# A trunk of two decoder layers on one core: one computed order for all engines, up products with tokens stationary, and seven products of quarters in part of the MLP

## The chip, the cores and the metric

The kernel runs on one core of a Trainium2 chip. The metric is the device time of one execution in microseconds. Work goes to TensorE (PE: matmuls, and PEld: loads of the stationary operand), VectorE (DVE), ScalarE (ACT), GpSimd (POOL) and the queues that issue DMAs, SyncE's (SP) above all.

## The reference, cut to what matters

256 tokens of width 2048 pass two layers, each a token mixer and an MLP on one residual stream.

```python
h = rms_norm(x, mix_norm_g[i])
x = x + (fox_attention if i % 2 == 0 else dilated_attention)(h, ...)
h = rms_norm(x, mlp_norm_g[i])
a = relu(h @ mlp_w_up[i])              # 256x2048 by 2048x8192
x = x + (a * a) @ mlp_w_down[i]        # 256x8192 by 8192x2048
```

Forgetting attention has 16 heads of 128 with normed q and k and a cumulative gate; dilated attention has 8 heads with three groups of q and k each and values of 256. All is float32. Of the multiplications nearly all lie in the projections: 12 + 4 units for the first mixer, 16 + 4 for the second, 32 + 32 for the MLPs, where a unit is 256 tokens by 2048 rows by 512 columns of a weight.

## The kernel before, in words

**Precision by parts.** A float32 operand is cut into a high part that TensorE's fast float32 form takes as it is (ACT casts it, L288) and a low part, the rest (DVE subtracts, L289). A product is three matmuls: high by high, high by low, low by high. The weights come in tiles of 256 rows by 512 columns (`raw`, loaded at L272 on SP's queue), and each tile is cut as a whole, 128x1024 per operation. Here such a tile is called a block pair, as it has two blocks of 128 rows (k). There are five buffers of raw tiles and five of cut ones.

**Three forms of product.** `product` (L317 to L319) keeps 128 tokens stationary and moves 512 weight columns: per k, two token halves by three matmuls of 512 columns. `product_transposed` (L365, L369) is used for the up projections: it keeps 128 weight columns stationary and moves tokens, so that its result already stands with hidden units on partitions, as the down projection needs it. Per k it takes four times one matmul of 512 columns (high weights by high and low tokens side by side) and one of 256. `last_product` (L343 to L345) is the last unit of all: it ends in parts, so that its additions and stores overlap, and its second half of tokens is in two runs of matmuls of 256 columns.

**An MLP** goes in four periods of 2048 hidden units: four up units, then four down units. `up_chain` (L842 to L852) adds the two halves of each bank, squares the positive part and cuts the result; the scale of the norm is applied as its square when the down product is added to x (L805).

**Order.** Python generators (`Jobs`) write the order by hand: each k step of a product is one tick, after which generators that have waited so many ticks emit their next instructions. What stands between the projections' matmuls on TensorE is attention (scores, transposes of probabilities, products with values) and transposes of normed tokens. Three of four chunks of a norm are turned from tokens on partitions to width on partitions by DVE in 32x32 squares (L399) and a way through DRAM (four writes and one read per 128 tokens); the last chunk by TensorE (L434). Queries and keys are turned through DRAM too (the reads on POOL's queue), except for two blocks by TensorE (L506). `behind` adds dependencies that fix one instruction behind another.

**Head.** The first weight tile comes in two loads of 256 KB on two queues and is cut in two halves (L915, L916).

Of the kernel before, what the change touches and what calls it, by code (L numbers as in the profile page):

```python
# [23 lines left out]
KC = D // P  # L24
DFF = 4 * D
# [9 lines left out]
RAW_BUFS = 5  # L35
W_BUFS = 5
W_SUB = 2
RAW_SUB = 2


class Jobs:

    def __init__(self):
        self.now = 0
        self.live = []
        self.done = set()  # L50
        self.running = False

    def spawn(self, gen):
        self.live.append([self.now, None, gen])
        if not self.running:
            self._run()

    def _run(self):
        self.running = True
        for job in list(self.live):  # L60
            while job[0] <= self.now and (job[1] is None or job[1] in self.done):
                try:
                    got = next(job[2])
                except StopIteration:
                    self.live.remove(job)
                    break
                if isinstance(got, int):
                    job[0], job[1] = self.now + got, None
                    if not got:
                        continue  # L70
                else:
                    job[1] = got
        self.running = False

    def tick(self):
        self.now += 1
        self._run()

    def need(self, key):
        tries = 0  # L80
        while key not in self.done:
            self.tick()
            tries += 1
            assert tries < 10000, key
# [3 lines left out]
def trunk(ctx: ExitStack, tc, x, fox_w_in, fox_b_f, fox_q_gain, fox_k_gain, fox_w_out, dil_w_in,  # L88
          dil_q_gain, dil_k_gain, dil_w_out, mix_norm_g, mlp_norm_g, mlp_w_up, mlp_w_down, out):
    nc = tc.nc  # L90
    jobs = Jobs()

    const = ctx.enter_context(tc.tile_pool(name="const", bufs=1))
    act = ctx.enter_context(tc.tile_pool(name="act", bufs=1))
    wpool = ctx.enter_context(tc.tile_pool(name="wpool", bufs=1))
    work = ctx.enter_context(tc.tile_pool(name="work", bufs=1))
    small = ctx.enter_context(tc.tile_pool(name="small", bufs=8))
    dram = ctx.enter_context(tc.tile_pool(name="dram", bufs=1, space=bass.MemoryType.DRAM))
    ps_acc = ctx.enter_context(tc.tile_pool(name="ps_acc", bufs=4, space=PSUM))
    ps_tp = ctx.enter_context(tc.tile_pool(name="ps_tp", bufs=2, space=PSUM))  # L100
    ps_sc = ctx.enter_context(tc.tile_pool(name="ps_sc", bufs=2, space=PSUM))


    warm = small.tile([P, 1], F32, tag="warm", name="warm", bufs=1)
    nc.gpsimd.memset(warm, 0.0)
    nc.scalar.activation(warm, warm, AF.Exp)
    ident = const.tile([P, P], F32, name="ident")
    make_identity(nc, ident)
    mhalf = const.tile([P, 8], F32, name="mhalf")
    nc.gpsimd.memset(mhalf, -0.5)  # L110


    spare = ps_sc.tile([P, P], F32, tag="sc", name="spare")

    def wake(times):
        for _ in range(times):
            nc.tensor.transpose(spare, ident, ident)

    wake(8)


    gain = const.tile([P, 4 * KC + 8], F32, name="gain")
    MLP_G, FOX_G, DIL_G = 2 * KC, 4 * KC, 4 * KC + 2

    def gain_rows(name, sources):
        rows = work.tile([2 * KC, P], F32, tag="s", name=name, bufs=4)
        at = 0
        for src in sources:
            nc.sync.dma_start(rows[at:at + src.shape[0], :], src)
            at += src.shape[0]  # L130
        return rows[0:at, :]

    def gain_columns(name, rows, at):
        n = rows.shape[0]
        ps = ps_tp.tile([P, 512], F32, tag="tp", name=f"ps_{name}")
        nc.tensor.transpose(ps[:, :n], rows, ident[:n, :n])
        return nc.vector.tensor_copy(gain[:, at:at + n], ps[:, :n])

    per_chunk = "l (c p) -> (l c) p"
    mix_rows = gain_rows("g_mix", [mix_norm_g.rearrange(per_chunk, p=P)])  # L140


    xt = [act.tile([P, NT, NC], F32, tag=f"x{n}", name=f"x{n}") for n in range(NX)]
    xv = x[0].rearrange("(t p) d -> p t d", p=P)


    bf = const.tile([P, FH], F32, name="bf")
    wfs = work.tile([P, KC, 2 * FH], F32R, tag="t1", name="wfs")
    tables = {}

    def distances():

        di = work.tile([P, 3 * P], I32, tag="s", name="di", bufs=4)
        nc.gpsimd.iota(di[:, 0:P], pattern=[[-1, P]], base=0, channel_multiplier=1)
        nc.gpsimd.iota(di[:, P:3 * P], pattern=[[-1, 2 * P]], base=P, channel_multiplier=1)
        return di

    def more_constants():
        yield 9
        wf = work.tile([P, KC, FH], F32, tag="t2", name="wf")  # L160
        with behind(issued["load"]):
            nc.sync.dma_start(wf, fox_w_in[0][:, 3 * D:3 * D + FH].rearrange("(c p) n -> p c n", p=P))
            nc.sync.dma_start(bf, fox_b_f.to_broadcast([P, FH]))
            qk_rows = gain_rows("g_qk", [fox_q_gain, fox_k_gain, dil_q_gain[0], dil_k_gain[0]])
            mlp_rows = gain_rows("g_mlp", [mlp_norm_g.rearrange(per_chunk, p=P)])
        di = distances()
        yield 6
        with behind(*issued["n0"]):
            nc.scalar.copy(wfs[:, :, 0:FH], wf)
            nc.vector.tensor_sub(wfs[:, :, FH:2 * FH], wf, wfs[:, :, 0:FH].bitcast(F32))  # L170
        jobs.done.add("wf")
        yield 1
        gain_columns("g_qk", qk_rows, FOX_G)
        for c in (FOX_G, DIL_G, DIL_G + 1, DIL_G + 2):
            nc.vector.tensor_scalar_mul(gain[:, c:c + 1], gain[:, c:c + 1], SCALE)
        yield 1
        gain_columns("g_mlp", mlp_rows, MLP_G)
        yield 1
        mask = work.tile([P, 3 * P], F32, tag="t0", name="mask")
        nc.vector.tensor_copy(mask, di)  # L180
        nc.vector.tensor_scalar(mask, mask, 0.0, None, ALU.is_ge)
        nc.vector.tensor_scalar(mask, mask, BIG, -BIG, ALU.mult, ALU.add)
        tables["mask"] = mask
        jobs.done.add("mask")

    def dilation_tables():
        di = distances()
        yield 2
        df = work.tile([P, 3 * P], F32, tag="s", name="df", bufs=4)
        nc.vector.tensor_copy(df, di)  # L190
        for g, r in enumerate(DILATION):
            t = work.tile([P, 3 * P], F32, tag=f"t{g}", name=f"dist{g}")
            ok = work.tile([P, 3 * P], F32, tag="s", name=f"ok{g}", bufs=4)
            nc.vector.tensor_scalar(ok, df, 0.0, None, ALU.is_ge)
            nc.vector.tensor_scalar(t, df, float(SPAN * r), None, ALU.is_le)
            nc.vector.tensor_mul(ok, ok, t)
            yield 1
            if r > 1:
                ri = work.tile([P, 3 * P], I32, tag="s", name=f"ri{g}", bufs=4)
                nc.vector.tensor_scalar(ri, di, r - 1, None, ALU.bitwise_and)  # L200
                nc.vector.tensor_copy(t, ri)
                nc.vector.tensor_scalar(t, t, 0.0, None, ALU.is_equal)
                nc.vector.tensor_mul(ok, ok, t)
                yield 1
            nc.vector.tensor_mul(t, df, ok)
            nc.vector.tensor_scalar(ok, ok, -BIG, BIG, ALU.mult, ALU.add)
            nc.vector.tensor_add(t, t, ok)
            tables[g] = t
            jobs.done.add(("table", g))
            yield 1  # L210


    plan = []

    def add(w, rows, cols):

        for r in range(rows[0], rows[1], RAW_SUB * P):
            plan.append((w, r, cols))

    for j in range(4):  # L220
        for part in range(3):
            add(fox_w_in[0], (0, D), [(part * D + j * NC, NC)])
    for n in range(NX):
        add(fox_w_out[0], (0, D), [(n * NC, NC)])

    def add_mlp(l):
        for b in range(4):
            for n in range(4):
                add(mlp_w_up[l], (0, D), [(b * D + n * NC, NC)])
            for n in range(NX):  # L230
                add(mlp_w_down[l], (b * D, (b + 1) * D), [(n * NC, NC)])

    add_mlp(0)
    for q4 in range(4):
        for g in range(3):
            c = g * DH * P + q4 * 2 * P
            add(dil_w_in[0], (0, D), [(c, 2 * P), (3 * DH * P + c, 2 * P)])
        add(dil_w_in[0], (0, D), [(6 * DH * P + q4 * NC, NC)])
    for n in range(NX):
        add(dil_w_out[0], (0, D), [(n * NC, NC)])  # L240
    add_mlp(1)

    issued = {}

    def behind(*instructions):
        stack = ExitStack()
        for i in instructions:
            stack.enter_context(tc.issue_after(getattr(i, "ins", i)))
        return stack

    def hold(first):

        if "held" not in issued:
# [737 lines left out]
```

## Time and profile before

| what | value |
|---|---|
| time, median of 3 runs (lowest to highest) | 2164.76 us (2164.07 to 2165.49) |
| profiled execution, first to last instruction | 2163.6 us |
| PE, PEld busy | 2153.5, 1918.3 us |
| DVE, ACT, POOL busy | 1395.5, 1108.1, 70.8 us |
| granted TensorE clock | 1.000 |
| moved by DMA | 454.11 MB |

The profiled execution's own time was not taken apart from its span; the median of the runs lies 1.2 us above the span. Matmuls overlap each other in the rows (a start every 0.2 us, a duration of 0.38), so PE's busy share says that something was in flight, not how fast the matmuls followed each other. For that, starts are compared.

### The profile page before, as it was taken

What the parts mean: (1) busy time and instruction counts of PE and PEld (TensorE: products, weight loads), DVE (VectorE), ACT (ScalarE), POOL (GpSimd) and SP (SyncE); (2) the same over time, 40 slices, a digit from 0 to 9 for tenths busy, and PEclk for the clock granted to TensorE, in tenths of its full rate; (3) what the DMA queues carried; (4) which work ended last, traced back from release to release, by engine and by line L of the source; (5) the groups of instructions that cost most, each with busy time, mean ns of one, the idle gap of its engine ahead of it and who ended that gap; (6) DMA issues with size and microseconds to landing.
All of it is one profiled execution on the core that took longest, in us unless ns stands there. A gap on an engine that the chain in (4) does not pass through costs nothing.

```text
span 2163.6 us, 30020 instructions
## 1 busy us (share of the span) xinstructions
PE 2153.5 (100%) x11251; PEld 1918.3 (89%) x11251; DVE 1395.5 (64%) x1847; ACT 1108.1 (51%) x1536; POOL 70.8 (3%) x87
## 2 busy tenths in 40 slices
PE   9999999999999999999999999999999999999999
PEld 8888888998998998998888888888988988988988
DVE  6777796665665565566667777766655655655664
ACT  6655655544444454455555555655544543544542
POOL 1111000000000000000010010000000000000000
PEclk9999999999999999999999999999999999999999
DMA  8676658666666766767776776767666666666764
GB/s 253 219 224 190 222 175 264 200 202 202 201 203 203 200 201 204 203 199 242 216 251 204 242 224 198 240 203 237 203 204 201 199 204 204 200 202 203 203 211 140
DMA packets 285683, 454.11 MB, mean 210 GB/s; under 512 B 21144, under 2 KB 99040, under 8 KB 285536
## 3 DMA queue, kind: packets, MB, share of 16 engines
q1 hardware_dynamic: 282240, 442.36, 65.7%
q0 software_dynamic: 2880, 9.44, 1.2%
q8 instruction: 88, 1.44, 0.3%
q10 hardware_dynamic: 416, 0.39, 0.1%
q14 instruction: 59, 0.48, 0.1%
HBM read 435.86 MB, written 16.25 MB: 209 GB/s over the span
## 4 chain that ended last, share of the span: by engine, by line
PE 95%; DVE 2%; ACT 1%; DMA 1%; issue 1%; POOL 0%; SPq 0%; ACTq 0%; DVEq 0%; POOLq 0%
PE acc L318 20%; PE acc L319 20%; PE acc L317 20%; PE up_n3a_acc L365 5%; PE up_n1a_acc L365 5%; PE up_n3a_tp L365 3%; PE up_n3a_sc L365 3%; PE up_n1a_tp L365 3%; PE up_n1a_sc L365 3%; PE up_n1a_acc L369 3%; PE up_n3a_acc L369 3%; PE up_n1a_sc L369 1%; PE up_n3a_sc L369 1%; PE up_n1a_tp L369 1%; PE up_n3a_tp L369 1%; DVE wl L289 1%
## 5 line engine op out<-in xcount | busy, mean ns | idle before, releaser
L289 DVE TENSOR_TENSOR wl<-raw,wh 128x1024 fp32r<-128x1024 f32 x799 | 974.8, 1223 | 692.2 <-ACT wh L288 690.1
L288 ACT CAST wh<-raw 128x1024 fp32r<-128x1024 f32 x799 | 837.2, 1048 | 924.1 <-PE acc L319 591.7
L317 PE MATMUL acc<-wh,hT_n 128*128 128x512 f32 x896 | 344.4, 385 | 0.0
L318 PE MATMUL acc<-wl,hT_n 128*128 128x512 f32 x896 | 340.1, 380 | 0.1
L319 PE MATMUL acc<-wh,hT_n 128*128 128x512 f32 x896 | 340.0, 380 | 0.0
L317 PE MATMUL acc<-wh,aTh_n1a 128*128 128x512 f32 x512 | 194.0, 379 | 0.0
L318 PE MATMUL acc<-wl,aTh_n1a 128*128 128x512 f32 x512 | 194.0, 379 | 0.0
L319 PE MATMUL acc<-wh,aTl_n1a 128*128 128x512 f32 x512 | 194.0, 379 | 0.0
L319 PEld LDWEIGHTS acc<-wh,hT_n 128*128 128x128 f32 x896 | 169.6, 189 | 24.1
L317 PEld LDWEIGHTS acc<-wh,hT_n 128*128 128x128 f32 x896 | 170.0, 190 | 22.6 <-ACT hT_n L440 0.7
L318 PEld LDWEIGHTS acc<-wl,hT_n 128*128 128x128 f32 x896 | 169.9, 190 | 22.3 <-DVE wl L289 0.5
L317 PE MATMUL acc<-wh,aTh_n3a 128*128 128x512 f32 x480 | 181.9, 379 | 0.0
L318 PE MATMUL acc<-wl,aTh_n3a 128*128 128x512 f32 x480 | 181.9, 379 | 0.0
L319 PE MATMUL acc<-wh,aTl_n3a 128*128 128x512 f32 x480 | 181.9, 379 | 0.0
L365 PE MATMUL up_n1a_acc<-hT_n,wh 128*128 128x512 f32 x512 | 181.6, 382 | 0.0
L365 PE MATMUL up_n3a_acc<-hT_n,wh 128*128 128x512 f32 x512 | 181.6, 382 | 0.0
L369 PE MATMUL up_n1a_acc<-hT_n,wl 128*128 128x256 f32 x512 | 139.6, 273 | 0.0
L369 PE MATMUL up_n3a_acc<-hT_n,wl 128*128 128x256 f32 x512 | 139.6, 273 | 0.0
L318 PEld LDWEIGHTS acc<-wl,aTh_n1a 128*128 128x128 f32 x512 | 96.8, 189 | 13.8
L319 PEld LDWEIGHTS acc<-wh,aTl_n1a 128*128 128x128 f32 x512 | 96.8, 189 | 13.7
L317 PEld LDWEIGHTS acc<-wh,aTh_n1a 128*128 128x128 f32 x512 | 96.8, 189 | 13.6
L365 PEld LDWEIGHTS up_n1a_acc<-hT_n,wh 128*128 128x128 f32 x512 | 96.8, 189 | 13.5
(730 smaller groups left out, 3209.4 us busy)
## 6 DMA issues: line engine op xcount, KB each, us to landing
raw<-in_mlp_w_up_dram SPq DMA_DIRECT2D x256, 512.0 KB, 4.0
raw<-in_mlp_w_down_dram SPq DMA_DIRECT2D x256, 512.0 KB, 3.7
raw<-in_dil_w_in_dram SPq DMA_DIRECT2D x192, 256.0 KB, 3.2
raw<-in_fox_w_in_dram SPq DMA_DIRECT2D x95, 512.0 KB, 4.1
raw<-in_fox_w_out_dram SPq DMA_DIRECT2D x32, 512.0 KB, 3.9
raw<-in_dil_w_in_dram SPq DMA_DIRECT2D x32, 512.0 KB, 6.6
raw<-in_dil_w_out_dram SPq DMA_DIRECT2D x32, 512.0 KB, 4.5
blocks_n<-turned_n SPq DMA_DIRECT2D x72, 64.0 KB, 1.9
```

Source lines behind the costliest of these rows:

```text
L288: issued["cast"] = nc.scalar.copy(hi, raw)
L289: issued["cut"] = nc.vector.tensor_sub(lo, raw, hi.bitcast(F32))
L317: nc.tensor.matmul(acc[t], ah[:, tok], hi, start=first, stop=False)
L318: nc.tensor.matmul(acc[t], ah[:, tok], lo, start=False, stop=False)
L319: issued["product"] = nc.tensor.matmul(acc[t], al[:, tok], hi, start=False, stop=last)
L365: issued["product"] = nc.tensor.matmul(banks[b], hi[:, i, col], in_turn(tokens.rearrange("p x s -> p (x s)"), P // 2), start=first, stop=last)
L369: nc.tensor.matmul(banks[b][:, 0:S], lo[:, i, col], in_turn(tokens[:, 0, :], P // 2), start=False, stop=False)
```

## The change

Nearly every line of the kernel is rewritten.

- **Order.** Each step is entered in a `Plan` with its engine, an estimated duration, what it reads and writes. `Plan.order` works backwards to a due time for each step, then runs a model of the five engines and the DMA queue three times, taking at each moment the ready step that is due first (attention's matmuls, marked urgent, before all). The instructions are then emitted in the order of the modelled times. Buffers are rings with fixed slots, and four phases share the memory.
- **Up products** keep tokens stationary, as all others. Their result has tokens on partitions: it is evacuated, scaled by the norm and passed through relu on ACT, turned by DVE (one operation of 1024) and through DRAM, squared, cast and cut.
- **Seven products of quarters.** In periods 1, 2 and 3 of both MLPs, in pairs 0, 2, 4, 5 and 7 of each up unit, the 256 tokens by 256 rows by 512 columns are taken as a 2x2 by 2x2 block product with sums of blocks (seven products instead of eight, each 128 tokens by 128 rows by 256 columns, three matmuls each). The other three pairs of those units use the same banks by quarters: eight products of 256 columns. In period 0 and in the down units nothing is halved.
- **Interleaving.** In periods 1 to 3, each up unit alternates with a down unit of the period before, pair by pair.
- **All norms' chunks** and all queries and keys after the first norm are turned through DRAM, on SP's queue.
- First units of a stage go in couples: six pairs of one, six of the other, then the two last pairs of each.
- The weights' first load is one of 512 KB. Buffers: six raw tiles and four cut pairs, one more of each in the MLPs.

```diff
+FIVE = (0, 2, 4, 5, 7)
+HALVED = [[(), (), (), ()], [FIVE] * 4, [FIVE] * 4, [FIVE] * 4]
...
+def moved(kb):
+    return kb / 380.0
...
+    HANDOFF = 0.25
+    LANDING = 2.1
...
+        def quarters(self, raw, keys, j, first, last):
+            q = S
+            hi, lo = cut(raw, keys, 0, 2 * NC, j in self.adding)
+            for i in range(2):
...
+                    for t in range(NT):
+                        a, b = (self.source.at(k, x, t) for x in range(2))
+                        for half in range(2):
+                            h, l = (in_turn(r(w)[:, i * NC + half * q:i * NC + (half + 1) * q], P) for w in (hi, lo))
+                            for m, w in ((a, h), (a, l), (b, h)):
+                                nc.tensor.matmul(to[t, half], m, w, start=False, stop=False)
...
+        def parts(self, raw, keys, j, first, last):
+            q = S
+            sums = raw_ring.take()
+            add("dve", on_dve(2 * q), lambda: nc.vector.tensor_add(
+                v(sums)[:, 0:2 * q].rearrange("p (g n) -> p g n", g=2),
+                v(raw)[:, q:3 * q].rearrange("p (g n) -> p g n", g=2),
+                v(raw)[:, 0:q].unsqueeze(1).to_broadcast([P, 2, q])), reads=keys, writes=[(sums, 0)])
+            hi_w, lo_w = cut(raw, keys, q, 3 * q)
+            add("dve", on_dve(q), lambda: nc.vector.tensor_add(v(sums)[:, 2 * q:3 * q], v(sums)[:, 0:q], v(raw)[:, 2 * q:3 * q]),
+                reads=[(sums, 0), *keys], writes=[(sums, 1)])
+            add("dve", on_dve(q), lambda: nc.vector.tensor_add(v(sums)[:, 3 * q:4 * q], v(sums)[:, 2 * q:3 * q], v(raw)[:, 3 * q:4 * q]),
+                reads=[(sums, 1), *keys], writes=[(sums, 2)])
+            hi_s, lo_s = cut(sums, [(sums, i) for i in range(3)], 0, 4 * q)
...
+                rows = [[(q1q5[:, 0:q], own(0, 0), pure, 0, 1), (q2q6[:, 0:q], own(1, 0), pure, 2, 1),
+                         (q3[:, 0:q], lambda x: at_sigma(x, 3), pure, 1, 3)],
+                        [(q1q5[:, q:2 * q], lambda x: at_sigma(x, 0), summed, 0, 2), (q7q4[:, 0:q], lambda x: at_sigma(x, 2), summed, 1, 1),
+                         (q2q6[:, q:2 * q], lambda x: at_sigma(x, 1), summed, 2, 2), (q7q4[:, q:2 * q], own(1, 1), summed, 3, 2)]]
+                for acc, a, w, at, edge in rows[summing]:
+                    nc.tensor.matmul(acc, a(0), w(0, at), start=first and edge & 1 == 1, stop=False)
+                    nc.tensor.matmul(acc, a(0), w(1, at), start=False, stop=False)
+                    nc.tensor.matmul(acc, a(1), w(0, at), start=False, stop=last and edge & 2 == 2)
...
+    def through_dram(turned, into, size=NT * NC):
+        blocks = blocks_ring.take()
+        for i in range(4):
+            def go(i=i):
+                nc.sync.dma_start(v(blocks)[:, :, :, i, :].rearrange("t j c x -> c t j x"),
+                                  v(turned)[32 * i:32 * i + 32, 0:size].rearrange("p (t j x) -> p t j x", t=NT, j=4))
+            add("dma", 0.45, go, reads=[turned], writes=[(blocks, i)])
...
+        add("dma", moved(512), back, reads=[(blocks, i) for i in range(4)], writes=[into])
...
+                for b_, to, at, names in pairs:
...
+                            nc.scalar.copy(flat(at()), two(v(b_)))
+                    add("act", on_act(NC), go, reads=[b_], writes=[(to, x) for x in names])
...
+                        nc.scalar.activation(at, at, AF.Relu, scale=by(t))
...
+            add("dve", 1.4, lambda: nc.vector.transpose(
+                v(turned).rearrange("p (t j b r) -> p t b j r", t=NT, j=4, b=4),
+                v(z)[:, 0:2 * NC].rearrange("p (t b j c) -> p t b j c", t=NT, j=4, c=32)),
+                reads=[(z, t) for t in range(NT)], writes=[turned, z])
+            through_dram(turned, z)
...
+    AC, BE = ("A0", "A1", "C0", "C1"), ("B0", "B1")
+    UU_D = "UUDUDUDUDUDUDUDD"
...
+                for u, d in zip(ups, downs):
+                    for c in UU_D:
+                        (u if c == "U" else d).block()
```

1722 lines of the change are left out of this document (945 added, 777 removed).

## Prediction

> **What bounds the kernel now.** I read the page first, then the two stretches of the trace that matter (projections alone, and attention), then single rows.
>
> ```profile
> span 2163.6 us, 30020 instructions
> PE 2153.5 (100%) x11251; PEld 1918.3 (89%) x11251; DVE 1395.5 (64%) x1847; ACT 1108.1 (51%) x1536; POOL 70.8 (3%) x87
> PEclk9999999999999999999999999999999999999999
> PE 95%; DVE 2%; ACT 1%; DMA 1%; issue 1%; POOL 0%; SPq 0%; ACTq 0%; DVEq 0%; POOLq 0%
> ```
>
> TensorE has a matmul in flight for 2153.5 of 2163.6 us at full clock, and 95% of the chain that ended last is its own work. So the time is the number of matmuls times their distance from start to start. Busy time cannot give that distance, since matmuls overlap; I take it from first and last rows of runs in the timeline. The columns are start, duration, engine, line.
>
> ```profile
> 1000.00 0.38 PE L317 MATMUL acc<-wh,aTh_n1a 128*128 128x512 f32 x1
> ...
> 1005.83 0.38 PE L317 MATMUL acc<-wh,aTh_n1a 128*128 128x512 f32 x1
> ```
> ```profile
> 449.91 0.38 PE L365 MATMUL up_n1a_acc<-hT_n,wh 128*128 128x512 f32 x1
> ...
> 452.20 0.38 PE L365 MATMUL up_n1a_tp<-hT_n,wh 128*128 128x512 f32 x1
> ```
> ```profile
> 2153.95 0.27 PE L343 MATMUL last<-wh,aTh_n3a 128*128 128x256 f32 x1
> ...
> 2159.20 0.28 PE L345 MATMUL last<-wh,aTl_n3a 128*128 128x256 f32 x1
> ```
>
> Down-type run: 27 steps in 5.83 us, 0.2159 us for 512 columns. Up run: seven couples of 512 and 256 columns in 2.29 us, 0.327 us a couple. Run of 256 columns alone: 47 steps in 5.25 us, **0.1117 us**, not half of 0.2159. This last row prices the change.
>
> Check of the whole: 68 units (of 2048 rows by 512 columns) with 96 matmuls of 512, less the 48 that the last unit splits: 6480 x 0.2159 = 1399; up, 32 units x 64 couples x 0.327 = 670; the split ones 11. Sum 2080. The other 84 us are attention, transposes, head, tail and short stalls.
>
> ```profile
> 660.00:990.00 330.00, 330.00 (x1778) 296.35 (x1777) 195.04 (x209) 152.12 (x176) 0.00 (x0) 1.00 0.66 202
> ```
> ```profile
> 40.00:320.00 280.00, 276.65 (x1389) 243.43 (x1388) 215.14 (x405) 166.01 (x295) 31.51 (x34) 1.00 0.65 204
> ```
> ```profile
> 1100.00:1400.00 300.00, 300.00 (x1483) 264.89 (x1482) 221.46 (x319) 172.76 (x260) 28.75 (x30) 1.00 0.72 226
> ```
>
> The stretches give length, PE, PEld, DVE, ACT, POOL busy, clock, DMA. In an MLP, VectorE is busy 59% (195 of 330); in the two attention stages 77% and 74%, and TensorE still loses only 3.35 us and 0.
>
> **The change, part by part.** *Matmuls.* A block pair is 256 rows by 512 columns. Up before: 8 couples, 8 x 0.327 = 2.617 us. After, in period 0 of each MLP (64 pairs): 12 x 0.2159 = 2.591. In periods 1 to 3, 72 pairs by quarters, 24 x 0.1117 = 2.681, and 120 pairs by seven products, 21 x 0.1117 = 2.346. Before 256 x 2.617 = 670.0; after 165.8 + 193.0 + 281.5 = 640.3. **Term 1: -29.7 us.** The saving of one eighth of the columns in 120 pairs is 39 us at half of 0.2159 each; a quarter of it goes to the dearer 256-column matmul.
>
> The Trainium skill, "TensorE: Matmul & The Clock Gate", section "LDWEIGHTS (loading the stationary operand)", puts a load of 128 columns at columns / 1.2, 107 ns, and its section "Back-to-back issue gap" a matmul of 256 columns at 262 cycles, 109 ns, so the load would just hide. The run above shows 0.1117, so the trace does not agree; by the pages Term 1 would be some 11 us larger.
>
> *Transposes on TensorE that go* to DMA: 24 of the norms before the two MLPs and the dilated layer, 16 of two key blocks.
>
> ```profile
> 384.24 0.44 PE ptx_n L434 x4
> ...
> 1390.80 0.44 PE tq_('dqk', 3, 2)_1_12903 L506 x4
> ```
>
> Ten groups of four at 0.44: **Term 2: -4.4 us.** What waits next there is the turn by DMA: the last chunk of a norm is now wanted only after twelve block pairs (31 us), and the turn takes two landings (rows below) and some 8 us of engine work, about 15.
>
> *VectorE in periods 1 to 3.* One up unit is interleaved with one down unit: 16 pairs. TensorE: 8 x 2.591 + 3 x 2.681 + 5 x 2.346 = 40.5 us (before 8 x 2.591 + 8 x 2.617 = 41.7); 24 such groups, 972 us. VectorE's own rate, start to start, from rows where it was never kept waiting:
>
> ```profile
> 1189.09 0.70 DVE L529 STREAM_TRANSPOSE sq_('dqk', 1, 1)_0_10872<-qn_('dqk', 1, 1)_0_10916 128x512 f32<-128x512 f32 x1
> 1189.71 0.67 DVE L529 STREAM_TRANSPOSE sq_('dqk', 1, 1)_1_10874<-qn_('dqk', 1, 1)_1_10919 128x512 f32<-128x512 f32 x1
> 1190.31 3.45 DVE L289 TENSOR_TENSOR wl<-raw,wh 128x1024 fp32r<-128x1024 f32 x3
> ```
> ```profile
> 301.36 0.75 DVE L579 TENSOR_TENSOR oTfl<-po_f,oTfh 128x256 fp32r<-128x256 f32 x2
> 302.02 0.41 DVE L589 TENSOR_TENSOR pTl_f<-ptp_f,pTh_f 128x256 fp32r<-128x256 f32 x1
> ```
> ```profile
> 320.54 1.28 DVE L807 TENSOR_TENSOR x<-x,acc 128x512 f32<-128x512 f32 x2
> ```
> ```profile
> L289 DVE TENSOR_TENSOR wl<-raw,wh 128x1024 fp32r<-128x1024 f32 x799 | 974.8, 1223 | 692.2 <-ACT wh L288 690.1
> L852 DVE TENSOR_TENSOR aTl_n3a<-z_n3a,aTh_n3a 128x512 fp32r<-128x512 f32 x32 | 21.8, 680 | 0.0
> ```
>
> 1024 elements: (3.45 - 1.23) / 2 = 1.11; 512: 1.28 - 0.68 = 0.60; 256: 0.66 / 2 = 0.33; 768 between: 0.86; a turn of 512: 0.62, so of 1024 some 1.2. A pair by seven products takes an addition of 512, a cut of 768, two additions of 256 and a cut of 1024: 0.60 + 0.86 + 0.66 + 1.11 = 3.23. Per group: 11 plain cuts 12.2; five such pairs 16.2; the end of the up unit and the addition to x 5.9 (0.60 + 0.66 + 1.20 in additions, turn 1.20, cut 1.11, x 1.11). Sum 34.3.
>
> ```profile
> 1145.50 0.54 DVE L773 TENSOR_TENSOR p_d<-sd 128x384 f32<-128x384 f32 x1
> 1146.07 0.56 DVE L774 TENSOR_TENSOR p_d<-p_d,sd 128x384 f32<-128x384 f32 x1
> 1146.55 1.22 DVE L289 TENSOR_TENSOR wl<-raw,wh 128x1024 fp32r<-128x1024 f32 x1
> ```
>
> An operation that reads its predecessor's result starts 0.57 after it, an independent one 0.48: 0.1 for each of some 14 dependent steps, 1.4. **VectorE needs 35.7 of 40.5 us, 88%**: it fits, above the 77% that cost nothing or little. It comes in bursts: at the start of a group, two up pairs and a down pair (7.6 us of TensorE) meet 5.5 us of cuts and most of the 5.9, a lag of about 3 us. Cover: five pairs of cut buffers. A group of one seven-product pair and one down pair takes three buffers in 4.94 us, so a buffer comes round in 8.2 us; the cut takes 2.6 (ScalarE 1.06, VectorE 1.23, handoffs), the matmuls on it 1.7 on average, leaving 3.9. Lag and cover nearly match. **Term 3**, stall in these 972 us: between the dilated stage's share, 0, and the attention stage's, 3.35 / 280 = 1.2%, or 11.6 us. I take the middle, **+5.8**, since some of the 3.35 belongs to attention's own chain. If the cover is gone each group loses the lag, 3 x 24 = 72 us. Below zero is excluded: 330.00 of 330.00 leaves nothing to regain.
>
> *ScalarE*, same group: 16 casts of 1024, five of 768, eight passes of 512, one more cast.
>
> ```profile
> L288 ACT CAST wh<-raw 128x1024 fp32r<-128x1024 f32 x799 | 837.2, 1048 | 924.1 <-PE acc L319 591.7 <-PE up_n1a_acc L365 150.1 <-PE up_n3a_acc L365 150.0
> L851 ACT CAST aTh_n3a<-z_n3a 128x512 fp32r<-128x512 f32 x32 | 20.0, 624 | 4.5 <-DVE z_n3a L848 4.4
> ```
>
> 17 x 1.05 + 5 x 0.84 + 8 x 0.62 = 27 of 40.5 us. The up unit has one set of four banks; its four evacuating passes (2.5 us) lie beside two down pairs (5.2 us). Nothing.
>
> *DMA.* Each up unit now goes through DRAM, four writes of 128 KB and one read of 512 KB, all on SP's queue between the weight loads.
>
> ```profile
> raw<-in_mlp_w_up_dram SPq DMA_DIRECT2D x256, 512.0 KB, 4.0
> ...
> blocks_n<-turned_n SPq DMA_DIRECT2D x72, 64.0 KB, 1.9
> turned_n<-blocks_n SPq DMA_DIRECT2D x18, 256.0 KB, 3.8
> ```
>
> 32 MB on 454, and the reads of the 20 query and key turns come from POOL's queue to SP's; per group five issues beside 16 loads. A read that waits for its writes holds the loads behind it for 2 us; seven raw buffers give 10 us and more. The turned result is wanted after 30 us or more. I cost it at nothing; if the cover went, a load would come 2 us late, once in a group: 48 us.
>
> *Attention under a computed order.* The same matmuls, placed between projections by estimated times instead of counted steps. Nothing in the trace shows such an order: a gain is at most the 3.35 us above, a loss as in the rivals. I take 0, by the dilated row.
>
> *Head.* First weights come in one load of 512 KB, not two of 256, so the first cast and cut are twice as long.
>
> ```profile
> 4.60 0.62 ACT L915 CAST wh<-raw 128x512 fp32r<-128x512 f32 x1 [1.84 <-DMA raw<-in_fox_w_in_dram]
> 5.25 0.69 DVE L916 TENSOR_TENSOR wl<-raw,wh 128x512 fp32r<-128x512 f32 x1 [0.82 <-ACT wh L915]
> ...
> 6.98 0.80 PE L317 MATMUL acc<-wh,hT_n 128*128 128x512 f32 x1
> ```
>
> 1.05 + 1.23 against 0.62 + 0.69: **Term 4: +1.0** (0 to 4, a late landing). The tail keeps its form: 0.
>
> Sum: 2163.6 - 29.7 - 4.4 + 5.8 + 1.0 = 2136.3. The median of the runs is 1.2 above the profiled span: **2137.5**.
>
> **The rivals.** *A, cheap quarters.* If 256 columns cost half of 512, 0.108, the 4248 of them (1728 and 2520) would save 16 us more than Term 1: 2121. For: in the up run a 256 beside a 512 adds 0.327 - 0.216 = 0.111, no more. Against: the run at 0.1117.
>
> *B, a stiff order.* In-order queues hold what stands behind a result that lands late. One load of 512 KB in the dilated stage took a median of 6.6 us:
>
> ```profile
> raw<-in_dil_w_in_dram SPq DMA_DIRECT2D x32, 512.0 KB, 6.6
> ```
>
> The order counts on 1.35 + 2.1 and one more us for a turned tile: 2.2 late. Behind 64 turns (32 up, 12 norm, 20 heads) at a third of that uncovered: +47 at worst, half of it likely: 2150 to 2163. Against: the consumers have ready work before and behind them.
>
> *C, slower: VectorE becomes the bound.* In the seven-product pair the second cut needs the third addition, then ScalarE's cast (1.06), then VectorE. If the queue holds nothing ready there, VectorE idles:
>
> ```profile
> 43.22 1.06 ACT wh L288
> 44.28 0.02 issue
> 44.30 1.23 DVE wl L289
> ```
>
> 1.08 each, 5.4 a group, and 2.4 at the unit's end (two passes of 0.62 before the turn, a cast before the last cut). All exposed: 35.7 + 7.8 = 43.5 us a group, +72: 2205. It costs nothing below 40.5 and turns the change slower from 40.5 + 33.1 / 24 = 41.9, that is with 6.2 of the 7.8 exposed. Taken most exposed, 2185. For: 88% and a lag like the cover. Against: the rows of three and four operations with no gap, wherever the queue has other work.
>
> The Trainium skill, "VectorE: DVE Perf Modes", section "The DRAIN you can't avoid", says that the next operation does not start until the pipe is empty, which speaks for C. The trace disagrees: three cuts in 3.45 us start 0.11 before their predecessor ends. By that rule the mean durations would add, 38.6 + 1.4 = 40.0 us a group, and no lag could be made up.
>
> **How the numbers follow.** Forecast (2125 to 2150) 0.63; A (2125 or less) 0.10; B 0.14, some of it within 0.2% or 4.3 us of before (about what a measurement of this kernel can tell from no change); C 0.13. Faster 0.83, same 0.04, slower 0.13. Range 2117 to 2168: A below, without Term 3's stall in part (2121 - 4), C from its threshold above; left out are 0.03 and 0.12.
>
> **What would show it.** Right: seven-product runs at 0.1117 a step; VectorE near 88% in the periods 1 to 3 with TensorE above 99% of its own rate; no group L434 or L506 after the head. Wrong: 0.108 a step (A); idle time of TensorE or VectorE ended by a DMA of a turned tile (B); VectorE's cut of the sums waiting on ScalarE while TensorE waits on that cut (C).

## The result, and the profile after

| | median | lowest to highest | profiled span |
|---|---|---|---|
| before, same chip | 2164.66 us | 2164.07 to 2165.49 | 2163.6 |
| changed | 2133.57 us | 2132.18 to 2134.92 | 2130.8 |

The ratio is 0.9856, with a 95% interval of 0.9842 to 0.9870: 31.1 us faster. The forecast was 2137.5, 3.9 too high. The page of the changed kernel, its total, engines and clock, then the shares of the chain that ended last:

```profile
span 2130.8 us, 32094 instructions
PE 2117.1 (99%) x12125; PEld 1917.1 (90%) x12125; DVE 1669.3 (78%) x2092; ACT 1263.0 (59%) x1640; POOL 57.3 (3%) x51
PEclk9999999999999999999999999999999999999999
PE 95%; DMA 2%; DVE 1%; issue 1%; ACT 1%; SPq 0%; DVEq 0%; ACTq 0%
```

VectorE has 274 us more to do and ScalarE 155 more, yet the chain is TensorE's as before. The time fell mainly because TensorE's own work became shorter. Its matmuls became more (12125 against 11251), many of them half as wide. The stretches of the changed kernel (length, PE, PEld, DVE, ACT, POOL busy, clock, DMA share, GB/s) show how well it is kept supplied:

```profile
460.00:860.00 400.00, 400.00 (x2705) 374.77 (x2705) 351.16 (x429) 251.59 (x295) 0.00 (x0) 1.00 0.72 233
40.00:320.00 280.00, 280.00 (x1417) 247.90 (x1416) 206.44 (x340) 156.02 (x253) 22.90 (x14) 1.00 0.68 212
1100.00:1400.00 300.00, 300.00 (x1482) 265.08 (x1481) 221.89 (x292) 169.21 (x242) 19.91 (x10) 1.00 0.71 227
```

The first line lies in periods 1 to 3 of an MLP: VectorE 351.16 of 400, 87.8%, and TensorE is never without a matmul. Nor did the matmuls follow each other more slowly than forecast: a group of 273 in 40.5 us would give 2696 in 400 us, and 2705 are there. The second is the first attention stage, in which 3.35 us had been lost before. Now the steps themselves, the changed kernel's timeline on TensorE (start, duration). A pair by quarters is followed by a down pair of 512 columns:

```profile
463.47 0.28 PE L403 MATMUL bank_C<-hi,hT 128*128 128x256 f32 x1
...
466.15 0.38 PE L384 MATMUL bank_E<-mlp_hi,aT 128*128 128x512 f32 x1
...
467.88 0.38 PE L386 MATMUL bank_E<-mlp_hi,aT 128*128 128x512 f32 x1
```

From 463.47 to 466.15 stand the 24 matmuls of a pair: 0.1117 us each, while the eight steps that follow take 1.73 us, 0.216 each. As before, half the columns take more than half the time.

What TensorE waits for over the whole span, in the changed kernel (us in total, times, longest), and then in the kernel before:

```profile
PE bank_E L666 <- DMA fox_s<-in_mix_norm_g_dram: 2.2, 1, 2.2
PE bank_B L384 <- DVE x L523: 2.0, 1, 2.0
PE bank_E L697 <- DMA x<-in_x_dram: 1.7, 1, 1.7
...
PE bank_A L384 <- issue: 1.4, 1, 1.4
PE bank_B L1192 <- DVE x L1207: 0.8, 1, 0.8
PE bank_A L384 <- ACT aT L642: 0.5, 1, 0.5
PE bank_C L403 <- DVE mlp_lo L346: 0.2, 1, 0.2
```
```profile
PE po_f L576 <- DVE pTl_f L589: 2.2, 3, 0.7
...
PE pc L674 <- DVE g_lf L671: 1.1, 1, 1.1
...
PE sc_d L610 <- DVE sd L759: 0.2, 1, 0.2
```

Attention's waits (2.2, 1.1 and 0.2, all of the kernel before) are gone but for 0.5 (aT L642). The MLPs' cuts cost 0.2 in all. In their place two things got worse. The head, in the timeline of TensorE:

```profile
6.75 0.31 PE L666 MATMUL bank_E<-ident,fox_s 32*128 32x32 f32 x1 [2.23 <-DMA fox_s<-in_mix_norm_g_dram]
8.78 1.09 PE L697 MATMUL bank_E<-ident,x 128*128 128x128 f32 x4 [1.72 <-DMA x<-in_x_dram]
9.51 0.78 PE L384 MATMUL bank_A<-hi,hT 128*128 128x512 f32 x1
```

The first product starts at 9.51, not 6.98, after waits for the gain rows and for the second half of x. That the gain rows do not set its start is shown by e9_wide_joints below. And the joints between stages, all engines:

```profile
378.18 0.45 PE L384 MATMUL bank_A<-mlp_hi,hT 128*128 128x512 f32 x1 [1.36 <-issue]
1030.62 1.21 DVE L523 TENSOR_TENSOR x<-x,bank_B 128x1024 f32<-128x1024 f32 x1
1031.97 0.45 PE L384 MATMUL bank_B<-hi,hT 128*128 128x512 f32 x1 [1.98 <-DVE x L523]
```

At 1031.97 the dilated stage begins on the bank pair that the MLP's last unit has just filled, and waits until VectorE has added that unit to x. At 378.18 it is the same with bank A after the first mixer's last unit. The two cost 1.36 and 1.98 us, and the last unit 0.8 more (L1192 in the waits). Behind the second one the granted clock is 0.50 for 3.4 us (row in the last section), some 1.7 us more.

### The profile page after: what moved, and what is told of

It is laid out like the page before. It is cut to its first block, busy times and chain, and to the rows that moved or that the text cites. A ratio compares the mean times of both kernels' runs of the same rounds, so it can differ in the third digit from the quotient of the medians.

```text
span 2130.8 us, 32094 instructions
## 1 busy us (share of the span) xinstructions
PE 2117.1 (99%) x12125; PEld 1917.1 (90%) x12125; DVE 1669.3 (78%) x2092; ACT 1263.0 (59%) x1640; POOL 57.3 (3%) x51
## 2 busy tenths in 40 slices
DMA packets 336140, 493.04 MB, mean 231 GB/s; under 512 B 21928, under 2 KB 137712, under 8 KB 335984
## 4 chain that ended last, share of the span: by engine, by line
PE 95%; DMA 2%; DVE 1%; issue 1%; ACT 1%; SPq 0%; DVEq 0%; ACTq 0%
PE bank_B L384 11%; PE bank_B L386 11%; PE bank_B L385 11%; PE bank_A L384 7%; PE bank_A L386 7%; PE bank_A L385 7%; PE bank_C L403 7%; PE bank_E L384 5%; PE bank_E L386 5%; PE bank_E L385 5%; PE bank_A L434 2%; PE bank_A L433 2%; PE bank_A L432 2%; PE bank_A L403 2%; PE bank_C L434 2%; PE bank_C L432 2%
## 5 line engine op out<-in xcount | busy, mean ns | idle before, releaser
L340 ACT CAST hi<-raw 128x1024 fp32r<-128x1024 f32 (+1 forms) x720 | 734.9, 1026 | 618.9 <-PE bank_B L386 211.5
L346 DVE TENSOR_TENSOR lo<-raw,hi 128x1024 fp32r<-128x1024 f32 (+1 forms) x720 | 852.7, 1192 | 295.4 <-ACT hi L340 283.2
L384 PE MATMUL bank_A<-hi,hT 128*128 128x512 f32 x520 | 199.2, 383 | 0.0
L384 PE MATMUL bank_B<-hi,hT 128*128 128x512 f32 x512 | 196.8, 384 | 2.0 <-DVE x L523 2.0
L386 PE MATMUL bank_A<-hi,hT 128*128 128x512 f32 x520 | 197.7, 380 | 0.0
L384 PE MATMUL bank_B<-hi,aT 128*128 128x512 f32 x520 | 197.7, 380 | 0.0
L385 PE MATMUL bank_A<-lo,hT 128*128 128x512 f32 x520 | 197.6, 380 | 0.0
L385 PE MATMUL bank_B<-lo,aT 128*128 128x512 f32 x520 | 197.1, 379 | 0.0
L386 PE MATMUL bank_B<-hi,aT 128*128 128x512 f32 x520 | 197.1, 379 | 0.0
L386 PE MATMUL bank_B<-hi,hT 128*128 128x512 f32 x512 | 194.8, 380 | 0.0
L385 PE MATMUL bank_B<-lo,hT 128*128 128x512 f32 x512 | 194.7, 380 | 0.0
L384 PE MATMUL bank_E<-hi,aT 128*128 128x512 f32 x408 | 154.8, 379 | 0.0
L386 PE MATMUL bank_E<-hi,aT 128*128 128x512 f32 x408 | 154.6, 379 | 0.0
L346 DVE TENSOR_TENSOR mlp_lo<-raw,mlp_hi 128x1024 fp32r<-128x1024 f32 (+1 forms) x108 | 126.9, 1175 | 32.8 <-ACT mlp_hi L340 29.7
L386 PEld LDWEIGHTS bank_A<-hi,hT 128*128 128x128 f32 x520 | 98.5, 189 | 14.5 <-DVE hT L707 0.5
L384 PEld LDWEIGHTS bank_A<-hi,hT 128*128 128x128 f32 x520 | 98.8, 190 | 13.2
```

Of the source, the lines that this page charges most:

```text
L340: add("act", on_act(n), lambda: nc.scalar.copy(r(hi)[:, 0:n], v(src)[:, at:at + n]), reads=keys, writes=[hi])
L346: add("dve", on_dve(n), lambda: nc.vector.tensor_sub(r(lo)[:, 0:n], v(src)[:, at:at + n], v(hi)[:, 0:n]), reads=[*keys, hi], writes=[lo])
L384: nc.tensor.matmul(acc, a, h, start=first and i == 0, stop=False)
L385: nc.tensor.matmul(acc, a, l, start=False, stop=False)
L386: nc.tensor.matmul(acc, b, h, start=False, stop=last and i == 1)
```

## The experiments

Each kernel was timed in five rounds beside the kernel before. Each is the changed kernel with the edit shown. First the size of the main term.

**No seven products** (e1_none).

```diff
-HALVED = [[(), (), (), ()], [FIVE] * 4, [FIVE] * 4, [FIVE] * 4]
+HALVED = [[()] * 4] * 4
```

> The changed kernel with no unit by seven products: all up units as whole products of 512 columns, the computed order, the tokens stationary and the turns by DMA as they are. Theory (the time is the sum of matmul steps, VectorE has room): 120 pairs cost 2.591 in place of 2.346 us, +29.4, and 72 pairs 2.591 in place of 2.681, -6.5: +22.9, so 2156.5. The rest of the change is then worth -8 against the kernel before. Rival (the gain comes from the computed order and the lost transposes, the seven products being eaten by the dearer small matmuls and by VectorE): within 5 us of the changed kernel, 2129 to 2139.

Measured: 2154.08 (2152.35 to 2155.10), ratio 0.9946 (0.9933 to 0.9958). So halving brings 20.5 of the 31.1 us. The step lengths of 0.2159 and 0.1117 give 23.0 for it (192 x 2.591 less 193.0 and 281.5). The other 10.6 us stay without any halving: 6.7 of them are the up products with tokens stationary by the same step lengths (256 x 2.617 less 256 x 2.591).

**Quarters as wide matmuls** (e2_wide). The accumulators are laid out anew so that the quarters that stand side by side share a bank; the three pairs of a unit that are not by seven products then take 512 columns at a time.

```diff
-                        for half in range(2):
-                            h, l = (in_turn(r(w)[:, i * NC + half * q:i * NC + (half + 1) * q], P) for w in (hi, lo))
-                            for m, w in ((a, h), (a, l), (b, h)):
-                                nc.tensor.matmul(to[t, half], m, w, start=False, stop=False)
+                        h, l = (in_turn(r(w)[:, i * NC:(i + 1) * NC], P) for w in (hi, lo))
+                        to = (q3q2, q0q4)[t]
...
+                                nc.tensor.matmul(to, m, w, start=False, stop=False)
```

> The accumulators lie so that the two column halves of one token half are neighbours in a bank, and the three other pairs of each halved unit are six matmuls of 512 columns a block in place of twelve of 256: same columns, half the number. Theory (a matmul of 256 columns alone costs 0.1117, more than half of 0.2159, as it is paced by something that counts matmuls, not columns): 72 pairs x (2.681 - 2.591) = -6.5, 2127.1. Rival (columns alone count): the same time, 2133.6.

Measured: 2125.86 (2123.95 to 2127.32), ratio 0.9814 (0.9800 to 0.9827): 7.7 us off for the same multiplications. 72 pairs at 2.681 less 2.591 give 6.5. The edit also gives the planner 6 x 0.216 for half such a pair in place of 12 x 0.109, so the order may have moved a little too. Against e1_none, which has no seven products and the same wide matmuls, the run is 28.2 us faster, and the 120 pairs by seven products had been priced at 29.4. A matmul has a price besides its columns. The Trainium skill, "TensorE: Matmul & The Clock Gate", section "Back-to-back issue gap", gives 109 ns for 256 columns, by which 24 of them would take 2.62 us and the edit would bring about 2 us, an estimate; the measurement speaks for 0.1117.

Next, how much room VectorE still has, and what ends it.

**All eight pairs, and six** (e3_eight, e4_six).

```diff
-FIVE = (0, 2, 4, 5, 7)
+FIVE = (0, 1, 2, 3, 4, 5, 6, 7)
```

> All eight pairs of the halved units by seven products. TensorE would need 39.5 us a group of 16 pairs, VectorE 8 x 1.11 + 8 x 3.23 + 5.9 + 2.0 = 42.6. Theory (VectorE bounds from about 40.5 us a group): a group takes 42.6 in place of 40.4, 24 x 2.2 = +53, 2186; at the least slower than the changed kernel. Rival (VectorE is far from its bound, its rows overlap more than worked out): 72 x 0.335 = -24, 2109.5.

```diff
-FIVE = (0, 2, 4, 5, 7)
+FIVE = (0, 2, 3, 4, 6, 7)
```

> Six of the eight pairs (0, 2, 3, 4, 6, 7) by seven products. TensorE 40.1 us a group, VectorE 10 x 1.11 + 6 x 3.23 + 5.9 + 1.6 = 38.0, 95%. Theory (VectorE fits while its need is below TensorE's): 24 x 0.335 = -8.0, 2125.6. Rival (88% with bursts is already the edge, the five cut buffers don't cover a longer lag): up to 1 us lost a group, 2133 to 2150.

Measured: eight 2238.10 (2229.56 to 2243.55), ratio 1.0329 (1.0307 to 1.0351); six 2153.92 (2151.14 to 2157.51), ratio 0.9946 (0.9933 to 0.9958). At eight the direction is the theory's and the loss larger. The stretch of eight, then of six, in the same columns as above:

```profile
460.00:860.00 400.00, 369.37 (x2338) 341.36 (x2337) 365.55 (x496) 240.32 (x288) 0.00 (x0) 0.95 0.67 210
```
```profile
460.00:860.00 400.00, 390.33 (x2590) 362.82 (x2589) 359.17 (x454) 250.28 (x295) 0.00 (x0) 0.99 0.70 226
```

TensorE loses 31 and 10 us in 400, and the granted clock is lower with it, yet VectorE is not full: 91% and 90%. At six its load is 35.7 + 3.23 - 1.11 = 37.8 us a group by the working above, of 40.2: it should fit, and the theory that only a full VectorE costs time fell. The timeline of six on VectorE shows a hole, and the waits from 620 to 666 us who pays (total us, times, longest):

```profile
658.47 1.21 DVE L523 TENSOR_TENSOR x<-x,bank_B 128x1024 f32<-128x1024 f32 x1
662.48 0.69 DVE L409 TENSOR_TENSOR mlp_raw<-raw 128x512 f32<-128x512 f32 x1 [2.80 <-DMA raw<-in_mlp_w_up_dram]
663.08 1.22 DVE L1010 TENSOR_TENSOR aT<-mlp_tr,aT 128x1024 fp32r<-128x1024 f32 x1
```
```profile
PE bank_E L386 <- DVE aT L1010: 2.9, 1, 2.9
```

An addition of a weight tile that has not landed stands at the head of VectorE's queue for 2.80 us. Behind it stands the low part of aT, which does not need that tile, and for which TensorE waits 2.9 us. Just before, ScalarE's queue has a hole of the same kind, on ScalarE and TensorE:

```profile
658.16 1.15 ACT L1003 ACTIVATE mlp_tr<-mlp_z 128x512 f32<-128x512 f32 x2 [1.92 <-DMA mlp_z<-blocks]
660.78 0.48 PE L384 MATMUL bank_E<-mlp_hi,aT 128*128 128x512 f32 x1 [2.22 <-ACT aT L1008]
```

Here the read of a turned tile had not landed, the high part of aT was cast late, and TensorE waited 2.22 us. Over the whole span of six the waits behind ScalarE's casts of aT are the larger of the two, 8.3 us (L1008) against 6.6 (L1010). Three guesses followed: more tiles loaded ahead, the planner's engine durations, and its landing time.

**Six, more raw tiles, fewer cut buffers** (e10_six_raw); **six, the planner's engine durations as measured** (e11_six_costs).

```diff
-MORE = (1, 1, 1)
+MORE = (3, 0, 0)
```

> Six pairs by seven products, as in the run that lost, with nine raw buffers in place of seven and four cut ones in place of five. Theory P (the loss came from raw buffers: each such pair holds two, a load starts too late, VectorE's addition waits for it and the cut of the down unit's activations stands behind): most of the loss goes, 2126 to 2136. Theory Q (the loss came from the order computed with VectorE taken as slower than it is): it stays, 2150 or above. Theory R (cut buffers): worse, 2160 or above.

```diff
-    return 0.24 + 0.00083 * n + (0.19 if accum else 0)
+    return 0.2 + 0.00074 * n + (0.1 if accum else 0)
...
-    return 0.17 + (0.00104 if inputs == 2 else 0.00054) * n
+    return 0.09 + (0.001 if inputs == 2 else 0.0005) * n
...
-            return 0.0 if a.eng == "pe" else 0.06
+            return 0.0
```

> Six pairs by seven products; the planner's durations are set to the measured distances from start to start (a cut of 1024: VectorE 1.11, ScalarE 0.96, no gap of 0.06 between operations), nothing else. Theory Q (the order was computed for a VectorE that needs more than TensorE, so its queue puts cuts that are due later ahead of the activations): the loss goes, 2125 to 2135. Theory P (raw buffers): it stays, 2145 to 2155.

Measured: e10_six_raw 2170.28 (2165.56 to 2174.73), ratio 1.0023 (1.0013 to 1.0032); e11_six_costs 2182.37 (2171.89 to 2183.95), ratio 1.0069 (1.0054 to 1.0084). Both are worse than plain six. As e10_six_raw also gave up a pair of cut buffers, it does not test more raw buffers alone. With the engine durations as measured, VectorE's waits for loads grow more than threefold; the waits from 460 to 860 us of e4_six, then of e11_six_costs:

```profile
DVE raw L409 <- DMA raw<-in_mlp_w_up_dram: 9.1, 10, 1.5
```
```profile
DVE raw L409 <- DMA raw<-in_mlp_w_up_dram: 31.4, 20, 3.7
```

So the order now counts on faster engines and on loads as early as before. That the slow durations had made up for the early landings is my reading of it; no run had true durations and true landings together.

**Six, a longer landing in the model** (e17_six_landing).

```diff
-    LANDING = 2.1
+    LANDING = 3.5
```

> Six pairs by seven products, and one number of the planner changed: it counts 3.5 us in place of 2.1 from the end of a DMA's transfer to its landing (with 1.35 of transfer: 4.85 us; the loads of 512 KB landed in 4.4 to 5.7). Theory S (the loss at six comes from VectorE's queue holding an addition on weights that land later than planned, at its head): the order puts these additions later and the loss goes, 2125 to 2136. Rival R (too few cut buffers for VectorE's lag, whatever the order): it stays, 2145 to 2160.

Measured: **2134.75** (2133.84 to 2135.78), ratio 0.9859 (0.9845 to 0.9872), 19.2 us better than six by one number. The work is the same; only its order moved. Its stretch, and VectorE's waits for the same loads in it; then ScalarE's waits for turned tiles in the stretch, of six and of this run:

```profile
460.00:860.00 400.00, 396.70 (x2658) 369.69 (x2657) 364.60 (x464) 254.45 (x302) 0.00 (x0) 1.00 0.73 233
```
```profile
DVE raw L409 <- DMA raw<-in_mlp_w_up_dram: 5.1, 6, 2.1
```
```profile
ACT mlp_tr L1003 <- DMA mlp_z<-blocks: 9.2, 6, 2.6
```
```profile
ACT mlp_tr L1003 <- DMA mlp_z<-blocks: 0.5, 2, 0.3
```

Six had come out 28.3 above what its theory gave, so the order's trust in early landings was the larger part of that. The one number stands for all DMAs. VectorE's waits for weights fell from 9.1 to 5.1 us, ScalarE's for turned tiles from 9.2 to 0.5, so the recorded theory, which names the weights alone, has at most a part of it; the two were not separated. The page of the changed kernel shows how far the trust went: the model takes 1.35 + 2.1 = 3.45 us for a load and for the read of a turned tile, where the medians are

```profile
raw<-in_mlp_w_up_dram SPq DMA_DIRECT2D x222, 512.0 KB, 4.4
...
mlp_z<-blocks SPq DMA_DIRECT2D x44, 512.0 KB, 5.6
```

**One pair of cut buffers fewer** (e6_fewer), with five pairs as in the changed kernel: what is the cover worth?

```diff
-MORE = (1, 1, 1)
+MORE = (1, 0, 0)
```

> The changed kernel (five pairs) with four cut buffers in place of five in the MLPs. Theory (the cover of five is 3.9 us against a lag of 3 us; with four a buffer comes round in 6.6 us, the cover is 2.3): 0.7 us lost a group, 24 x 0.7 = +17, 2150. Rival (VectorE lags less than worked out): 2134.

Measured: 2155.39 (2152.10 to 2163.49), ratio 0.9963 (0.9953 to 0.9974): 21.8 us lost with one buffer pair. The waits from 460 to 860 us name it, TensorE waiting for a cut, which the changed kernel has in no row there:

```profile
PE bank_A L433 <- DVE lo L346: 5.3, 4, 2.1
```

Over the whole span such waits are 16.6 us. e10_six_raw gave up the same pair, which fits its loss of 16.4 against plain six, though its waits lie on aT (16.8 us over the span) as well as on cuts.

**Up and down apart** (e7_apart): eight up pairs, then eight down pairs.

```diff
-    UU_D = "UUDUDUDUDUDUDUDD"
+    UU_D = "UUUUUUUUDDDDDDDD"
```

> Five pairs, but each up unit's eight pairs run in one piece and then the down unit's eight. Theory (88% of VectorE fits only because down pairs, cheap for it, lie between): during the up pairs VectorE needs 16.2 + 3.3 of cuts and some 5 of the unit's end against 19.8 us of TensorE, and works ahead by at most 5 us of buffers: 1 to 5 us lost a group, 2158 to 2250. Rival (the mean load decides, the mixture doesn't matter): 2134.

Measured: 2146.91 (2141.51 to 2148.74), ratio 0.9909 (0.9896 to 0.9923): 13.3 us lost, less than the theory, more than its rival. Alternating matters, but less than the theory's 1 to 5 us a group. That the planner, which orders the other engines around any sequence, saves the rest is a guess.

The last group tries for a faster kernel.

**Wide quarters, other banks at one joint, gain rows first** (e9_wide_joints): e2_wide and

```diff
-            add("dma", 0.1, go, writes=[(rows, i)])
+            add("dma", 0.1, go, writes=[(rows, i)], urgent=name == "mix")
...
-        units = [Unit(source, w, 0, [(n * NC, NC)], next_banks(), add_to_x(n, then)) for n in range(NX)]
+        units = [Unit(source, w, 0, [(n * NC, NC)], next_banks() if n < NX - 1 else ("E0", "E1"), add_to_x(n, then)) for n in range(NX)]
```

> Wide quarters, and three small waits removed: the gain rows are loaded ahead of the second half of x (TensorE's first product started at 9.5 us, the gain rows landed at 6.7), and the last unit of each output projection uses the banks E0 and E1, so that no stage begins on the banks that the stage before has just filled (1.4 us lost at 376, 2.0 at 1030). Theory (each wait is on the chain, nothing else is late behind it): 2125.9 - 1.9 - 1.4 - 2.0 = 2120.6. Rival (the next wait takes their place: first weights, or x's addition itself): 2124 to 2126.

Measured: **2122.31** (2120.77 to 2124.84), ratio 0.9804 (0.9792 to 0.9817), the fastest of all. The step from e2_wide is 3.6 us by the medians, of the 5.3 expected, and the intervals of the two ratios overlap. The waits at the two joints are gone from its trace. The head gained nothing, as the rival had it: the gain rows are there earlier, yet the first product starts at 9.56 us (9.13 in e2_wide, 9.51 in the changed kernel), behind one wait of 3.79 us that ends on the first tile's cut.

**Seven products in period 0 too** (e18_period0): e9_wide_joints with pairs 0 and 7 of the four period-0 units, on two sets of banks in turn.

```diff
-HALVED = [[(), (), (), ()], [FIVE] * 4, [FIVE] * 4, [FIVE] * 4]
+HALVED = [[(0, 7)] * 4, [FIVE] * 4, [FIVE] * 4, [FIVE] * 4]
...
-                banks = AC if halved else ("A0", "A1") if b or n % 2 == 0 else ("B0", "B1")
+                banks = (AC if b or n % 2 == 0 else ("B0", "B1", "E0", "E1")) if halved else ("A0", "A1") if b or n % 2 == 0 else ("B0", "B1")
```

> Wide quarters and the three small waits removed, and in period 0 too, pairs 0 and 7 of each up unit by seven products, its units on two sets of four banks in turn. Theory (VectorE has 17.9 of 20.2 us to do there, the sums of tokens are ready in time): 16 pairs x 0.245 = -3.9 on 2122.3, 2118.4. Rival (the norm's turn and the token sums at the start of the MLP already fill VectorE, or the first units wait for them): 2122 to 2130.

Measured: 2168.33 (2166.07 to 2170.29), ratio 1.0016 (1.0007 to 1.0025). Theory and rival both missed. Its waits from 440 to 500 us:

```profile
PE bank_E L384 <- ACT mlp_z L972: 15.6, 1, 15.6
...
ACT mlp_tr L1006 <- DMA mlp_z<-blocks: 10.4, 1, 10.4
```

TensorE stands 15.6 us before banks that are evacuated (L972) into z. There is one z tile, and it was still on its way through DRAM for the unit before. Both MLPs have such a wait, 31.2 us together of the 46.0 lost against e9_wide_joints. That reading comes from this trace alone; no run with a second z was made.

**Six with everything that helped** (e21_six_all): e9_wide_joints, six pairs, landing 3.5.

```diff
-FIVE = (0, 2, 4, 5, 7)
+FIVE = (0, 2, 3, 4, 6, 7)
...
-    LANDING = 2.1
+    LANDING = 3.5
```

> Six pairs, the planner's landing at 3.5 us, wide quarters and the three small waits removed. Theory (what is left of the loss at six, some 9 us in the run with the later landing, is VectorE's lag at 91% and more, and stays): 2122.3 - 24 x 0.245 + 9 = 2125. Rival (it was the order alone, and this order has no such places): 2122.3 - 5.9 = 2116.4, the fastest.

Measured: 2143.32 (2138.68 to 2144.60), ratio 0.9893 (0.9877 to 0.9910), worse than both its parts. Its profile spreads the loss over waits for cuts, aT and evacuated banks, 3 to 5 us each. Why the parts do not add stays open.

## Why the prediction was right

**Term 1, -29.7: held.** The steps are 0.1117 and 0.216 in the changed kernel as in the kernel before. Taking the halving away cost 20.5 (23.0 by the terms), making quarters wide brought 7.7 (6.5), and between these two runs lie 28.2 (29.4). Rival A, cheap quarters, is out: at half of 0.2159 wide quarters would have brought nothing.

**Term 2, -4.4: held in kind.** The groups of transposes at L434 and L506 of the kernel before are gone, and no wait of TensorE for a turned tile stands in the waits above. Its own time was not measured apart.

**Term 3, +5.8: the step that failed.** The prediction took the middle between the dilated stage's share of stall, 0, and the attention stage's. It measured 0 in the stretch of 400 us quoted above, and 0.2 in the MLPs' waits over the whole span. VectorE's load was right (88% against 87.8%), and lag and cover were as near each other as the working had them: one cut buffer less costs 21.8 us. What was wrong was to charge the MLPs with half of a stall that belonged to attention's own chain: in the waits of the kernel before, 2.2 us stand behind the cut of probabilities (L589) and 1.1 behind the gate (L671).

**Attention, at 0: a little was left out.** Of the 3.5 us that TensorE had waited there, 0.5 is left, near the best that the prediction had allowed (3.35). Which part of the new order brings it was not separated.

**Term 4, +1.0: held by its size, not by its working.** The first product came 2.5 us later, but that is not what the head cost. A step of the first products takes 0.43 us in both kernels, until it falls to 0.22 at 11.35 us before and at 12.63 after, so the early start was worth half. By 33.5 us the kernel before had issued 96 matmuls of products and the changed kernel 92: 4 x 0.216, 0.9 us. What the working had only in its range (0 to 4) is the landing. ScalarE's first cast waits for the whole tile and starts at 6.54, not at 4.60, and VectorE's cut of that tile ends at 8.85, not at 5.94:

```profile
6.54 1.04 ACT L340 CAST hi<-raw 128x1024 fp32r<-128x1024 f32 x1 [4.24 <-DMA raw<-in_fox_w_in_dram]
7.62 1.23 DVE L346 TENSOR_TENSOR lo<-raw,hi 128x1024 fp32r<-128x1024 f32 x1
```

The second half of x comes at the same time in the changed kernel, so the two are not separated there; in e9_wide_joints TensorE's wait ends on the cut.

**Not foreseen: joints**, 2.0, 1.4 and 0.8 us in the waits, and 1.7 of half clock behind the first of these.

**The sum, and luck.** Worked on the span, the forecast was 2136.3 against 2130.8. Of these -5.5 us, Term 3 gives -5.8, attention -3.0, the head -0.1, the joints and their clock +5.9; the other -2.5 are not assigned, of which 0.8 is a shorter tail behind the last matmul (3.3 us against 4.2). The median lies 2.8 above the span and not 1.2, which gives +1.6. So Term 1, which carries the change, was right on its own, while the total came within 3.9 us with luck: 8.9 us too high in some places stood against 7.5 too low in others.

**Rival B, a stiff order,** did not happen here and happened at six pairs: the same late landings, 19.2 us. Its price of up to 47, half of it likely, was of the right size; its condition was incomplete. In the changed kernel's stretch VectorE has waits for late weights too (7.5 and 5.6 us, below), and they cost TensorE nothing, while ScalarE waits only 0.4 us for turned tiles, against 9.2 at six. That it takes late landings and an engine with no slack behind them, VectorE at 94% by the working, is a reading; the load was not varied with the order held.

```profile
DVE lo L346 <- ACT hi L340: 26.4, 43, 1.4
...
DVE raw L409 <- DMA mlp_raw<-in_mlp_w_up_dram: 7.5, 4, 3.4
...
DVE raw L409 <- DMA raw<-in_mlp_w_up_dram: 5.6, 7, 1.7
```

**Rival C, VectorE as the bound,** did not happen at five, and at eight it is not shown. At five VectorE's waits for ScalarE's casts are 26.4 us in 400 (first row), of the 7.8 a group feared some 2.7, and all are covered. At eight the working gives 42.1 us a group against TensorE's 39.5; 42.1 for 40.5 us in 24 groups would be 38 us, but 104.5 were lost against the changed kernel, with VectorE busy 91%. C's own sign, TensorE waiting for a cut, is small there: 13.5 us over the span (hi and lo). The most, 60.8 us, are waits for banks that ScalarE evacuates late (L969). The waits of eight from 460 to 860 us, then the longest of them in the timeline, on ScalarE and TensorE:

```profile
PE bank_A L432 <- ACT mlp_z L969: 21.1, 4, 7.9
```
```profile
546.95 1.15 ACT L1003 ACTIVATE mlp_tr<-mlp_z 128x512 f32<-128x512 f32 x2 [4.11 <-DMA mlp_z<-blocks]
548.00 0.57 ACT L969 COPY mlp_z<-bank_A 128x512 f32<-128x512 f32 x1
548.62 0.58 PE L432 MATMUL bank_A<-mlp_hi,hT 128*128 128x256 f32 x1 [7.86 <-ACT mlp_z L969]
```

ScalarE stood 4.11 us before a turned tile that had not landed; the evacuation stands behind it in its queue and writes the same z tile. All four waits of the stretch follow such a wait of ScalarE (4.11, 2.07, 2.29 and 2.48 us, 10.95 of TensorE's 21.1). So at eight, as at six and in e18_period0, rival B's late turned tile is a large part of the loss. How much of the rest is VectorE's need, and how much the order, was not separated.

## What to carry to other kernels

Price a matmul by its distance from start to start at its own width: halving the columns left 0.1117 of 0.2159 us, so seven products of halves save 9% of a pair and not 12.5%, and what is not by seven products is better left wide. In a fixed order of in-order queues, set the planner's landing times to the late end of what the DMA rows show before making its engine times exact: at six pairs the first brought 19.2 us, the second alone cost 28.5. Then read the rows in which an engine that has other work waits for a load or for a turned tile. Before taking the cover of buffers as ample, or using the last tenth of an engine, take one buffer away: here it cost 21.8 us.

## What the runs showed of the hardware

Behind many of TensorE's single waits of about 2 us or more, the granted clock fell to 0.50 for 3.4 us or longer, and a step of 512 columns then took 0.43 us. In the changed kernel this stands behind the joint at 1031.97, in the columns of the stretches:

```profile
1033.00:1036.40 3.40, 3.40 (x10) 2.69 (x9) 0.44 (x3) 0.34 (x2) 0.70 (x1) 0.50 0.81 197
```

Over the span the mean was 0.999 in the changed kernel, 0.976 at eight (waits of up to 7.9 us) and 0.989 in e18_period0 (two of 15.6). Many short waits alone did not do it: e11_six_costs waits 33 times for cuts, 33.8 us in all and none over 2.5, and kept 0.999. At eight this is at most 0.024 x 2241.8 = 54 us, an estimate, as part of the slow clock falls into waits. Together with the 86.5 us of TensorE's waits in its MLPs it covers what eight lies above the sum of its steps: 134 us, the profiled run's 2243.6 less the 2109.5 that its rival gave.

The changed kernel moved 493.04 MB, mean 231 GB/s, against 454.11 and 210, and its loads of 512 KB landed in medians of 4.4 to 5.7 us.
